# Scan of an RWKV-7 layer: inverses by 16x16 blocks and TensorE, loads and exponentials one pair ahead, 14 chunk tiles

## Chip, cores, metric

The kernel runs on one core of a Trainium2 chip, in float32. The metric is the device time of one execution in microseconds; three executions give the median. The profile is that of one more execution.

## The reference

One inference step of a two-layer trunk: 512 latent tokens and 128 context tokens, width 1024. Layer 0 mixes tokens by a bidirectional RWKV-7 scan, layer 1 by neighbourhood attention; a squared-ReLU MLP follows each. The change touches the scan alone. For each of 16 heads and both directions the reference runs, token by token, on a 64x64 state:

```python
def step(S, inp):
    r_t, w_t, k_t, v_t, kk_t, a_t = inp
    sa = jnp.einsum('bhvk,bhk->bhv', S, -kk_t)
    S_new = (S * w_t[:, :, None, :] + sa[..., None] * (kk_t * a_t)[:, :, None, :]
             + v_t[..., None] * k_t[:, :, None, :])
    y = jnp.einsum('bhvk,bhk->bhv', S_new, r_t)
    return S_new, y
```

## The kernel before, in words

The scan is not run token by token but in chunks of 32. Five steps n = 0 to 4 each take one tile of 128 tokens forward and one backward (n = 0 is the context, the rest the latent tokens); a tile has four chunks, e = 0 to 3. Within a chunk the tokens depend on one another through a lower triangular 32x32 matrix for each head and direction, whose inverse is needed: 128 of them for each n.

**Preparation.** A step n has eight units (half of the heads `hg`, direction `d`, half of the tile `i`; two units with the same `hg` and `d` are a pair). `prep_elem` loads a pair's inputs on SP's queue (lines 890 to 894), makes the running sum of the log decays on DVE (line 896), two exponentials on ACT (897, 898) and products on POOL: KB (912, 913) for the pair, and for each unit a chunk tile C (927). Half of C is filled with zeros first, on ACT (919) and POOL (922), so that a product over all 128 rows picks one head. `prep_group`, twice a unit, multiplies KB by C on TensorE (line 942 by the helper of line 832, tile `pp`), copies the triangular matrices to `invA` (952) and the rest into C (954, 957). After the eighth unit `invert` computes the inverses on DVE (lines 964 to 978): a mask, a transpose of 32x32 blocks, then forward substitution with one multiplication and one addition for each column, split in two from the 11th column on, 100 operations, and a transpose into TT.

**Order.** `fill(k)` does up to k groups, and units as far as there are free C tiles. During the value projection (`tm_product`, line 239) each of 20 output tiles calls `fill(2)`. There are 16 C tiles, eight for even and eight for odd n; twelve of them exist in that stage, so twelve units are done there. In the recurrence `phase_scan` calls `fill` with 0, 1, 1, 2 in each e; two C tiles for each direction come free after every second e.

**Recurrence.** For each n, e and direction `chain_step` does: a state product R on TensorE (16 products of 128x32 tiles, tile A), its copy Rc on ACT (1015), U = TT x Rc on TensorE (16 products of 32x32 tiles), four copies of U into the state tile GU on ACT (1032), the state update on TensorE (16 products of 64x64 tiles, tile B) and its copy on ACT (1088) or with a decay on DVE (1086, 1091), and the output product Y. Once the recurrence runs, every product of helper `mm` (line 832) is tied behind the one before it by a dependency, so TensorE's order there is the order of the program. Between the products stand adaLN products (`adaraw`), whose small addition is line 300 on DVE. Finished tiles are normalised in `post_half`, on DVE, POOL and ACT. After n = 4 `wo_first` begins the output projection (line 1199), with residual buffers `wr` filled on ACT's queue (1195, 1196) and stored on SP's (1202).

The order on DVE, ACT and POOL follows the program as far as a planner's estimate lets it; all four queues run in order.

Of the kernel before, what the change touches and what calls it, by code (L numbers as in the profile page):

```python
# [16 lines left out]
P = 128  # L17
D = 1024
# [154 lines left out]
class K:  # L173
# [534 lines left out]
    def c_slots(self, pool, n, par):  # L708

        for i in range(n):  # L710
            c = pool.tile([P, 26, 64], F32, name=f"C{i}")
            self.nc.any.tensor_copy(c[:, 16:18, :].rearrange("p a x -> p (a x)"), self.cst("ident"))
            self.free[par].append(c)

    def scan_pools(self, st):
        pool = lambda name, bufs, **k: self.pool(st, name, bufs, **k)
        self.ld = pool("ld", 1, side="right")
        self.el = pool("el", 2, side="right")
        self.kbp = pool("kbp", 4, side="right")
        self.ttp = pool("ttp", 2, side="right")  # L720
        self.inv = pool("inv", 1, side="right")
# [9 lines left out]
        self.free = [[], []]  # L731
# [4 lines left out]
        self.steps = [{"tiles": t, "C": {}, "par": i % 2} for i, t in enumerate(((4, 4), (0, 3), (1, 2), (2, 1), (3, 0)))]  # L736
# [3 lines left out]
        self.pin = False  # L740

# [11 lines left out]
    def phase_scan(self, st):  # L753
        nc, tc = self.nc, self.tc
        if True:
# [32 lines left out]
            for n, ts in enumerate(self.steps):  # L788
                for e in range(4):
                    s0, s1 = (self.chain_step(ts, n, e, d) for d in range(2))  # L790
# [72 lines left out]
    def fill(self, n):  # L863

        for i in range(n + 1):
            while self.e_i < len(self.units) and self.e_i <= self.m_i + 2 and self.free[self.units[self.e_i][0]["par"]]:
# [12 lines left out]

    def prep_elem(self, ts, hg, d, i):  # L880

        nc = self.nc
        if "FC" not in ts:
            ts["FC"] = self.fcp.tile([P, 2, 2, 2, 4], F32, name="FC")
        ww = (i, 1 - i)[d]
        tt = ts["tiles"][d]
        rev = (lambda a: a[:, :, :, ::-1]) if d else (lambda a: a)
        if i == 0:
            wi = self.el.tile([P, 520], F32, name="wi")
            nc.sync.dma_start(wi, self.tz_d[d][tt, :, hg])  # L890
            dd = self.ld.tile([P, 1024], F32, name="ld_d")
            nc.sync.dma_start(dd, self.dd_d[d][tt, :, hg])
            sh = self.ld.tile([P, 1024], F32, name="ld_s")
            nc.sync.dma_start(sh, self.sh_d[tt, :, hg])
            w = self.el.tile([P, 520], F32, name="w")
            nc.vector.tensor_tensor_scan(wi, self.cst("scan1"), wi, 0.0, ALU.mult, ALU.add)
            nc.scalar.activation(w, wi, AF.Exp, scale=-0.5 * EXPM)
            nc.scalar.activation(wi, wi, AF.Exp, scale=0.5 * EXPM)
            w, wi = (a.rearrange("p (q w t) -> p q w t", w=2, t=65) for a in (w, wi))
            nc.gpsimd.tensor_copy(ts["FC"][:, d, :, :, 2 * hg:2 * hg + 2].rearrange("p w b l -> p l b w"),  # L900
                                  w[:, :, :, 64].rearrange("p (l b) w -> p l b w", b=2))
            self.pe_in = w, wi, dd, sh
# [12 lines left out]
        C = ts["C"][d, hg, ww] = self.free[ts["par"]].pop(0)  # L915
# [652 lines left out]
```

## Time and profile before

| | us |
|---|---|
| median of three executions | 2249.48 (2247.16 to 2249.74) |
| profiled execution, its own time | 2250.36 |
| profiled execution, span | 2248.5 |
| value projection with the first preparation | 302 to 411 of the span |
| recurrence | 411 to 797 |
| first part of the output projection | 798 to 845 |

The span runs from the first to the last instruction of the profiled execution. Engines are named PE (TensorE matmul), PEld (its weight load), DVE (VectorE), ACT (ScalarE), POOL (GpSimd) and SP (SyncE, which issues DMAs). A product in float32 is issued as two instructions.

### The profile page before, as it was taken

Reading aid. Unit: us, or ns where it says so; the run is one execution under the profiler, and the core shown is the slowest. Engines: PE = TensorE matmul, PEld = TensorE weight load, DVE = VectorE, ACT = ScalarE, POOL = GpSimd, SP = SyncE. Lnnn points to the kernel's source line nnn. Section 1 sums busy time; section 2 is a strip of 40 time slices with the busy share of each in tenths; the row PEclk is TensorE's granted clock in tenths of the full one; section 3 lists DMA queues with packets and bytes.
Section 4 is the critical chain, followed back from the end, with each engine's and each line's share of the span. In section 5 each row is a group of like instructions: output and inputs, shape, how many; then the busy total and the mean of one; then the engine's idle time right before and its main releaser. Section 6 shows DMA issues by size and latency. Waiting matters only on the chain.

```text
span 2248.5 us, 44838 instructions
## 1 busy us (share of the span) xinstructions
PE 2007.7 (89%) x18516; PEld 1823.6 (81%) x18516; DVE 1180.0 (52%) x2587; ACT 866.0 (39%) x1735; POOL 463.8 (21%) x558
## 2 busy tenths in 40 slices
PE   5898978757665677999999999999999999999999
PEld 3787877646554566999999998888777999999999
DVE  6847667396687766433333334434566643434342
ACT  3544554356553425413131323221576331313130
POOL 0001257566552323101010110000232210101010
PEclk9897989888888798999999999999899999999999
DMA  6454864444443455323232223433311232222221
GB/s 232 123 154 140 251 204 158 141 149 148 131 130 121 101 181 164 94 75 113 76 104 75 94 75 114 137 116 108 111 58 29 75 123 75 75 76 74 74 75 70
DMA packets 161388, 260.01 MB, mean 116 GB/s; under 512 B 46880, under 2 KB 103328, under 8 KB 161184
## 3 DMA queue, kind: packets, MB, share of 16 engines
q1 hardware_dynamic: 146816, 240.37, 34.2%
q10 hardware_dynamic: 14368, 16.78, 2.3%
q8 instruction: 145, 2.38, 0.4%
q14 instruction: 59, 0.48, 0.1%
HBM read 218.18 MB, written 37.35 MB: 114 GB/s over the span
## 4 chain that ended last, share of the span: by engine, by line
PE 73%; DVE 13%; DMA 6%; ACT 3%; POOL 2%; issue 2%; SPq 1%; ACTq 0%; DVEq 0%; POOLq 0%
PE psl L205 53%; PE psl L239 4%; PE ps L1495 2%; DVE invT L973 2%; DVE invX L976 2%; PE po L1532 2%; PE pp L832 2%; POOL C L927 2%; PE pt L1520 2%; DVE C L957 1%; PE psl L286 1%; DMA ld_s<-scr 1%; PE pp L1199 1%; DMA wi<-scr 1%; PE st L548 1%
## 5 line engine op out<-in xcount | busy, mean ns | idle before, releaser
L191 ACT CAST whi<-wraw 128x1024 fp32r<-128x1024 f32 x179 | 187.2, 1048 | 730.9 <-PE psl L205 702.5
L205 PE MATMUL psl<-xh,whi 128*128 128x320 f32 (+1 forms) x1712 | 419.8, 318 | 20.8 <-ACT whi L191 15.1
L205 PE MATMUL psl<-xl,whi 128*128 128x320 f32 (+1 forms) x1712 | 417.0, 316 | 7.9 <-DVE xl L248 7.9
L205 PE MATMUL psl<-xh,wlo 128*128 128x320 f32 (+1 forms) x1712 | 415.0, 315 | 2.6 <-DVE wlo L193 2.6
L205 PEld LDWEIGHTS psl<-xh,whi 128*128 128x128 f32 x1712 | 295.4, 192 | 39.4 <-ACT whi L191 19.3
L205 PEld LDWEIGHTS psl<-xl,whi 128*128 128x128 f32 x1712 | 296.3, 192 | 13.9 <-DVE xl L248 10.0
L205 PEld LDWEIGHTS psl<-xh,wlo 128*128 128x128 f32 x1712 | 297.1, 192 | 5.2 <-DVE wlo L193 3.0
L1152 DVE SCALAR_TENSOR_TENSOR xres<-psl,mods,xres 128x320 f32<-128x320 f32 (+2 forms) x216 | 81.7, 434 | 305.5 <-PE psl L205 305.5
L1315 POOL TENSOR_TENSOR relu<-relu 128x640 f32<-128x640 f32 x64 | 80.8, 1263 | 753.1 <-ACT relu L1314 736.2
L205 PE MATMUL psl<-hhh,wlo 128*128 128x320 f32 x1024 | 233.5, 309 | 0.0
L205 PE MATMUL psl<-hhh,whi 128*128 128x320 f32 x1024 | 233.2, 309 | 0.0
L205 PE MATMUL psl<-hhl,whi 128*128 128x320 f32 x1024 | 233.2, 309 | 0.0
L193 DVE TENSOR_TENSOR wlo<-wraw,whi 128x1024 fp32r<-128x1024 f32 x179 | 222.5, 1245 | 14.2 <-ACT whi L191 14.0
L205 PEld LDWEIGHTS psl<-hhh,whi 128*128 128x128 f32 x1024 | 171.2, 188 | 0.4 <-issue 0.4
L205 PEld LDWEIGHTS psl<-hhl,whi 128*128 128x128 f32 x1024 | 171.1, 188 | 0.0
L205 PEld LDWEIGHTS psl<-hhh,wlo 128*128 128x128 f32 x1024 | 171.1, 188 | 0.0
L1272 DVE TENSOR_TENSOR relu<-psl,rms_b 128x320 f32<-128x320 f32 x128 | 60.7, 486 | 144.4 <-PE psl L205 143.3
L832 PE MATMUL pp<-C,KB 128*64 128x128 f32 x1280 | 97.6, 298 | 27.2 <-DVE C L957 13.1
L248 DVE TENSOR_TENSOR hhl<-relu,hhh 128x640 fp32r<-128x640 f32 x64 | 53.4, 834 | 127.9 <-ACT hhh L247 127.8
L832 PEld LDWEIGHTS pp<-C,KB 128*64 128x64 f32 x1280 | 79.9, 149 | 41.3 <-issue 20.7
L957 DVE TENSOR_TENSOR C<-pp,cstsb 64x512 f32<-64x512 f32 x80 | 55.1, 689 | 76.5 <-ACT C L954 68.9
L1032 ACT ACTIVATE GU<-A 32x256 f32<-32x256 f32 x160 | 60.0, 375 | 84.3 <-DVE mods L300 51.8
(288 smaller groups left out, 3389.7 us busy)
## 6 DMA issues: line engine op xcount, KB each, us to landing
wraw<-in_mlp_w SPq DMA_DIRECT2D x128, 512.0 KB, 3.5
adaraw<-in_ada_w SPq DMA_DIRECT2D x96, 512.0 KB, 4.9
ld_d<-scr SPq DMA_DIRECT2D x20, 512.0 KB, 4.1
ld_s<-scr SPq DMA_DIRECT2D x20, 512.0 KB, 3.9
bias<-in_bias SPq DMA_DIRECT2D x16, 384.0 KB, 3.5
scr<-ta SPq DMA_DIRECT2D x16, 325.0 KB, 3.5
wi<-scr SPq DMA_DIRECT2D x20, 260.0 KB, 4.5
scr<-bp SPq DMA_DIRECT2D x16, 320.0 KB, 4.6
```

What stands on the lines that cost most here:

```text
L191: nc.scalar.copy(hi, raw)
L193: nc.vector.tensor_tensor(lo, raw, hi.bitcast(F32), op=ALU.subtract)
L205: self.nc.tensor.matmul(ps[g][:, :e - c], lhsT=a[:, k, :], rhs=b[:, c:e], start=(k == 0 and j == 0), stop=(k == n - 1 and j == 2))
L239: nc.tensor.matmul(ps, lhsT=a[:, tc_], rhs=w, start=(k == 0 and j == 0), stop=(k == KT - 1 and j == 2))
L248: (lo_eng or nc.vector).tensor_tensor(xl, src, xh.bitcast(F32), op=ALU.subtract)
L832: r = (op or self.nc.tensor.matmul)(*a, **k)
L927: nc.gpsimd.tensor_tensor(rev(o) if s == 0 else o, v4(sh, s, ww)[hs], f[hs], op=ALU.mult)
L957: nc.vector.tensor_tensor(C[o, 8 * h:8 * h + 8, :], pn[o, :, 0:64], mask[o], op=ALU.mult)
L1032: nc.scalar.activation(gu[64 - 64 * hp:96 - 64 * hp, hp, pp].rearrange("p b v -> p (b v)"), U[32 * q:32 * q + 32, :], AF.Copy, scale=-0.5)
L1152: nc.vector.scalar_tensor_tensor(out[:, a:b], ps[g][:, o:o + b - a], gate[:, k, j:j + 1], x[:, a:b], op0=ALU.mult, op1=ALU.add)
L1272: nc.vector.tensor_tensor(t[:, c], ps[q][:, :HALF], rb[:, c], op=ALU.mult)
L1315: nc.gpsimd.tensor_tensor(t, t, t, op=ALU.mult)
```

## The change

1. `invert` solves only the two 16x16 diagonal blocks on DVE, both in one operation: 14 multiplications and 14 additions. The off-diagonal block comes from TensorE in two rounds of 128 products of 32x32 tiles with 16 columns (`invert_rest`), with a copy on ACT between them and an addition on DVE behind them; one more transpose on DVE and three zero fills on POOL prepare the operands. The rounds are called from `fill`, the first before the third group after the inverse was issued, or else before the first U that needs them.
2. Loads, running sum and exponentials of a pair are issued with the pair before it; the running sums of the pair after next are loaded then, too. The input buffers are doubled.
3. There are 14 chunk tiles (8, 2 and 4), from which any n may take, within limits at the end; the zero halves and their fills go, and the products of KB with C use 64 rows of the array each.
4. In `wo_first` two residual buffers take the place of three.

```diff
     def c_slots(self, pool, n, par):
+        ident = self.cst("ident")
         for i in range(n):
-            c = pool.tile([P, 26, 64], F32, name=f"C{i}")
-            self.nc.any.tensor_copy(c[:, 16:18, :].rearrange("p a x -> p (a x)"), self.cst("ident"))
+            c = pool.tile([P, 25, 64], F32, name=f"C{i}")
+            self.nc.vector.tensor_tensor(c[:, 16], ident[:, :64], ident[:, 64:], op=ALU.add)
...
+    def room(self, ts, hg, d, i):
+        n = ts["n"]
+        first = (0, 1, 1 - i, i, 0)[n]
+        for j in (first,) if n == 4 or n == 3 and i else (first, 1 - first):
+            if self.free[j]:
+                return j
...
-        self.c_slots(self.pool(self.cst1, "c1", 1, side="right"), 4, 1)
+        self.inv = prep("inv", 1)
+        self.kbp = prep("kbp", 4)
+        self.el = prep("el", 2)
+        self.ld = prep("ld", 2)
+        self.c_slots(prep("c1", 1), 2, 1)
...
     def fill(self, n):
...
+            self.invert_on()
             u = self.units[self.m_i]
             self.prep_group(*u, self.m_g)
...
+    def decays(self, p):
...
+        nc.vector.tensor_tensor_scan(tz, self.cst("scan1"), tz, 0.0, ALU.mult, ALU.add)
+        nc.scalar.activation(w, tz, AF.Exp, scale=-0.5 * EXPM)
+        nc.scalar.activation(wi, tz, AF.Exp, scale=0.5 * EXPM)
...
     def prep_elem(self, ts, hg, d, i):
...
+            self.load_rk(p + 1)
+            self.decays(p + 1)
+            self.load_tz(p + 2)
+            self.pe_in = *self.w_in.pop(p), *self.rk_in.pop(p)
...
-        for h in range(2):
-            z = C[64 - 64 * h:P - 64 * h, 8 * h:8 * h + 8, :]
-            if h:
-                nc.scalar.activation(z.rearrange("p a b -> p (a b)"), self.cst("scan1")[64 - 64 * h:P - 64 * h, :512],
-                                     AF.Copy, scale=0.0)
-            else:
-                nc.gpsimd.memset(z, 0.0)
...
-                self.mm(pv[r:r + 64, e, q, :], lhsT=KB[:, q, e].rearrange("p s t -> p (s t)"), rhs=C[:, n:17 + h:16 + h - n, :],
-                        start=True, stop=True, tile_position=(0, r))
+                self.mm(pv[r:r + 64, e, q, :], lhsT=KB[hs, q, e].rearrange("p s t -> p (s t)"), rhs=C[hs, n:17:16 - n, :],
+                        start=True, stop=True, tile_position=(64 * h, r))
...
     def invert(self, ts):
...
+        nc.gpsimd.memset(Xm[:, 16:32, 0:16], 0.0)
+        nc.gpsimd.memset(Dt[:, :, 0:16], 0.0)
...
+        for s in range(1, 15):
+            m = 15 - s
+            t = tmp[:, :2 * m * s].rearrange("p (b m s) -> p b m s", b=2, m=m)
+            nc.vector.tensor_tensor(t, Xd[:, :, s + 1:, s:s + 1].broadcast_to([P, 2, m, s]),
+                                    Xd[:, :, s:s + 1, 0:s].broadcast_to([P, 2, m, s]), op=ALU.mult)
+            nc.vector.tensor_tensor(Xd[:, :, s + 1:, 0:s], Xd[:, :, s + 1:, 0:s], t, op=ALU.add)
+        nc.vector.transpose(ST.rearrange("p n s -> p s n"), Xm.rearrange("p t s -> p s t"))
+        nc.gpsimd.memset(ST[:, :, 16:32], 0.0)
...
+        self.inv_todo = ts, self.invert_rest(Dt, ST, TT)
+        self.inv_wait = 3
+
+    def invert_rest(self, D, ST, TT):
+        nc = self.nc
+        pz = self.pp_tile()
...
+        for n in range(32):
+            for q in range(4):
+                self.mm(z[32 * q:32 * q + 32, n], lhsT=D[32 * q:32 * q + 16, n, :], rhs=ST[32 * q:32 * q + 16, n, 0:16],
+                        start=True, stop=True, tile_position=(32 * q, 32 * q))
+        nc.scalar.copy(ST[:, :, 0:16], z)
+        yield
+        for n in range(32):
+            for q in range(4):
+                qs = slice(32 * q, 32 * q + 32)
+                self.mm(w[qs, n], lhsT=ST[qs, n, :], rhs=TT[qs, n, 16:32], start=True, stop=True,
+                        tile_position=(32 * q, 32 * q))
+        nc.vector.tensor_tensor(TT[:, :, 16:32], TT[:, :, 16:32], w, op=ALU.add)
+
+    def invert_on(self, ts=None):
+        if ts is None:
+            self.inv_wait -= 1
+            if self.inv_todo and self.inv_wait <= 0 and next(self.inv_todo[1], 1):
+                self.inv_todo = None
+        while ts is not None and self.inv_todo and self.inv_todo[0] is ts:
+            if next(self.inv_todo[1], 1):
+                self.inv_todo = None
...
     def chain_step(self, ts, n, e, d):
...
         yield
+        self.invert_on(ts)
         TT = ts["TT"]
...
     def wo_first(self, adp):
...
-            xi = self.wf[min(k % 3, 1)].tile([P, NA], F32, name=f"wr{k % 3}")
+            xi = self.wf[k % 2].tile([P, NA], F32, name=f"wr{k % 2}")
```

## Rows read from the trace of the kernel before

**Rows 1.** Page, part 1: busy us (share of the span) xinstructions.
```profile
PE 2007.7 (89%) x18516; PEld 1823.6 (81%) x18516; DVE 1180.0 (52%) x2587; ACT 866.0 (39%) x1735; POOL 463.8 (21%) x558
```

**Rows 2.** Stretch, us, busy us (instructions) of PE PEld DVE ACT POOL, clock, DMA: stages.
```profile
302.00:411.00 109.00, 93.64 (x882) 86.03 (x886) 73.62 (x158) 48.65 (x118) 71.42 (x98) 0.94 0.52 159
411.00:798.00 387.00, 247.50 (x6309) 199.94 (x6298) 271.50 (x726) 192.15 (x489) 190.61 (x252) 0.81 0.45 134
```

**Rows 3.** Busy times of the recurrence: n = 4, and the sum of all five.
```profile
733.20:797.00 63.80, 37.77 (x986) 32.00 (x982) 42.10 (x105) 27.00 (x61) 22.48 (x21) 0.73 0.41 105
sum 385.50, PE 246.51 PEld 199.31 DVE 270.25 ACT 190.85 POOL 190.15; mean PE 49.30 PEld 39.86 DVE 54.05 ACT 38.17 POOL 38.03
```

**Rows 4.** Busy times of single steps of the recurrence.
```profile
522.70:536.60 13.90, 12.03 (x344) 9.84 (x344) 5.98 (x10) 9.97 (x28) 8.56 (x14) 1.00 0.57 183
606.50:620.40 13.90, 11.97 (x340) 9.72 (x340) 5.59 (x9) 9.97 (x28) 8.65 (x14) 1.00 0.61 189
620.40:646.30 25.90, 14.52 (x340) 12.16 (x340) 22.56 (x64) 12.21 (x33) 10.32 (x17) 0.74 0.33 105
661.80:678.10 16.30, 13.03 (x352) 10.06 (x340) 8.33 (x13) 10.78 (x30) 6.43 (x10) 0.90 0.57 181
678.10:693.60 15.50, 12.18 (x340) 9.81 (x340) 5.77 (x11) 7.59 (x22) 1.04 (x1) 1.00 0.38 121
747.40:760.00 12.60, 8.55 (x268) 7.12 (x270) 11.16 (x32) 4.91 (x12) 1.04 (x1) 0.89 0.19 43
```

**Rows 5.** Timeline: start us, us, engine, line [idle before <-releaser]; two stretches.
```profile
603.67 1.15 PE L832 MATMUL B<-GU,C 64*64 64x64 f32 x32
...
604.75 1.10 PE L832 MATMUL A<-GU,C 128*32 128x64 f32 x64
...
606.96 0.65 PE L832 MATMUL A<-Rc,TT 32*32 32x64 f32 x32 [1.10 <-ACT Rc L1015]
...
614.45 1.97 PE L832 MATMUL pp<-C,KB 128*64 128x128 f32 x32
...
626.00 0.31 DVE L973 TENSOR_TENSOR invT<-invX 128x30 f32<-128x30 f32 x2
...
637.87 1.07 PE L832 MATMUL A<-Rc,TT 32*32 32x64 f32 x32 [9.71 <-ACT Rc L1015]
...
821.43 4.41 PE L1199 MATMUL pp<-wx,ww 128*128 128x384 f32 x24 [1.28 <-DVE wr L1201]
```

**Rows 6.** Waits in the recurrence: engine, line, waited for: us, times, longest.
```profile
ACT GU L1032 <- DVE mods L300: 51.8, 16, 13.0
...
ACT w L897 <- DVE wi L896: 29.2, 5, 11.4
...
PE A L832 <- DVE TT L978: 16.2, 3, 13.0
```

**Rows 7.** Groups in the recurrence: busy us, mean ns of one | idle before.
```profile
L973 DVE TENSOR_TENSOR invT<-invX 128x108 f32<-128x108 f32 (+14 forms) x200 | 61.5, 335 | 0.9
...
L976 DVE TENSOR_TENSOR invX<-invX,invT 128x38 f32<-128x38 f32 (+14 forms) x200 | 59.7, 324 | 1.0
...
L919 ACT ACTIVATE C<-cstsb 64x512 f32<-64x512 f32 x28 | 17.2, 628 | 1.5 <-PE A L832 1.2
...
L922 POOL MEMSET C<- 64x512 f32 x28 | 14.5, 523 | 7.2 <-PE A L832 6.9
...
L978 DVE STREAM_TRANSPOSE TT<-invX 128x1024 f32<-128x1024 f32 x4 | 7.7, 1931 | 0.1
```

**Rows 8.** The same with the shapes kept apart: two shapes of line 973.
```profile
L973 DVE TENSOR_TENSOR invT<-invX 128x90 f32<-128x90 f32 x12 | 4.2, 353 | 0.0
...
L973 DVE TENSOR_TENSOR invT<-invX 128x110 f32<-128x110 f32 x12 | 2.8, 263 | 0.0
```

**Rows 9.** Waits in the stage before the recurrence.
```profile
PE psl L239 <- ACT vhi L228: 8.3, 2, 4.9
```

**Rows 10.** DMA issues: KB each, median us to landing.
```profile
scr<-wr SPq DMA_DIRECT2D x8, 192.0 KB, 3.1
```

More of the change, by code (lines that the diff above doesn't have):

```diff
@@ L729, in scan_pools @@
             self.gu_zero(self.gu[d][0])
[L731 removed]
+        self.free, self.home = [[], []], {}
         self.c_slots(pool("c0", 1, side="right"), 8, 0)
         self.cst1 = st.enter_context(ExitStack())
[L734 removed]
+        prep = lambda name, bufs: self.pool(self.cst1, name, bufs, side="right")
+        self.inv = prep("inv", 1)
[3 more added lines that the diff above has]
+        self.c_slots(prep("c1", 1), 2, 1)
         self.late = False
[L736 removed]
+        self.steps = [{"tiles": t, "C": {}, "n": i} for i, t in enumerate(((4, 4), (0, 3), (1, 2), (2, 1), (3, 0)))]
+        self.pairs = [(s, hg, d) for s in self.steps for hg in range(2) for d in range(2)]
         self.units = [(s, hg, d, i) for s in self.steps for hg in range(2) for d in range(2) for i in range(2)]
@@ L865, in fill @@
         for i in range(n + 1):
-            while self.e_i < len(self.units) and self.e_i <= self.m_i + 2 and self.free[self.units[self.e_i][0]["par"]]:
+            while self.e_i < len(self.units) and self.e_i <= self.m_i + 2 and self.room(*self.units[self.e_i]) is not None:
                 self.prep_elem(*self.units[self.e_i])
@@ L878, in fill, with load_tz, load_rk @@
                     self.invert(u[0])
+    def load_tz(self, p):
+        if p < len(self.pairs):
+            ts, hg, d = self.pairs[p]
+            tz = self.tz_in[p] = self.el.tile([P, 520], F32, name="tz")
+            self.nc.sync.dma_start(tz, self.tz_d[d][ts["tiles"][d], :, hg])
+    def load_rk(self, p):
+        if p < len(self.pairs):
+            ts, hg, d = self.pairs[p]
+            tt = ts["tiles"][d]
+            dd = self.ld.tile([P, 1024], F32, name="ld_d")
+            self.nc.sync.dma_start(dd, self.dd_d[d][tt, :, hg])
+            sh = self.ld.tile([P, 1024], F32, name="ld_s")
+            self.nc.sync.dma_start(sh, self.sh_d[tt, :, hg])
+            self.rk_in[p] = dd, sh
@@ new lines, in decays @@
+    def decays(self, p):
+        nc = self.nc
+        if p >= len(self.pairs):
+            return
+        ts, hg, d = self.pairs[p]
+        if "FC" not in ts:
+            ts["FC"] = self.fcp.tile([P, 2, 2, 2, 4], F32, name="FC")
+        tz = self.tz_in.pop(p)
+        w = self.el.tile([P, 520], F32, name="w")
+        wi = self.el.tile([P, 520], F32, name="wi")
+        nc.vector.tensor_tensor_scan(tz, self.cst("scan1"), tz, 0.0, ALU.mult, ALU.add)
+        nc.scalar.activation(w, tz, AF.Exp, scale=-0.5 * EXPM)
+        nc.scalar.activation(wi, tz, AF.Exp, scale=0.5 * EXPM)
+        w, wi = (a.rearrange("p (q w t) -> p q w t", w=2, t=65) for a in (w, wi))
+        nc.gpsimd.tensor_copy(ts["FC"][:, d, :, :, 2 * hg:2 * hg + 2].rearrange("p w b l -> p l b w"),
+                              w[:, :, :, 64].rearrange("p (l b) w -> p l b w", b=2))
+        self.w_in[p] = w, wi
@@ L880, in prep_elem @@
     def prep_elem(self, ts, hg, d, i):
         nc = self.nc
-        if "FC" not in ts:
-            ts["FC"] = self.fcp.tile([P, 2, 2, 2, 4], F32, name="FC")
+        p = self.e_i // 2
         ww = (i, 1 - i)[d]
-        tt = ts["tiles"][d]
         rev = (lambda a: a[:, :, :, ::-1]) if d else (lambda a: a)
         if i == 0:
[L889 to L902, printed above, removed]
@@ L1051, in chain_step @@
         if e % 2 == 1:
-            self.free[ts["par"]] += [ts["C"].pop((d, hg, ww)) for hg in range(2)]
+            for hg in range(2):
+                c = ts["C"].pop((d, hg, ww))
+                self.free[self.home[id(c)]].append(c)
         yield
```

51 lines of the change are left out of this document (29 added, 22 removed).

## The prediction

> **What bounds the kernel now.** I read the page first: PE is busy for 89% of the span [rows 1]. The busy times by stage show that this share hides a stretch of another kind: in the 109 us in which the value projection runs beside the first scan preparation PE is busy for 93.6 us at a clock of 0.94, in the 387 us of the recurrence for 247.5 us at 0.81, with DVE at 271.5, ACT at 192 and POOL at 191 [rows 2]. No engine fills the recurrence, so it is a chain of waits, and I cut it into its 20 steps, from one copy of R in the forward direction (line 1015) to the next. They add up to 385.5 us, 19.3 us each, of which 63.8 us belong to the last four, n = 4 [rows 3].
>
> The steps are not alike [rows 4]. Four that hold four groups of preparation and no inverse take 13.9, 13.9, 16.3 and 15.5 us; PE is busy for 12.0 to 13.0 us of them and its clock stands at 0.90 to 1.00. The step beside an inverse takes 25.9 us: DVE is busy for 22.6 us of it, PE for 14.5 us with the clock down to 0.74. A step without groups takes 12.6 us. So outside the inverses TensorE's own order sets the pace, and inside them DVE does.
>
> The timeline shows the mechanism once [rows 5]: PE stands still for 9.71 us before the U product at 637.87 us, which then takes 1.07 us for its 32 instructions; the same product at 606.96 us took 0.65 us. The list of waits names the kinds [rows 6]: ACT waits 51.8 us for the small addition of line 300 and 29.2 us for the running sum of line 896, both queued on DVE among the inverse's operations, and everything on ACT (the copies of R, U and the state) is behind those waits; PE waits 16.2 us for TT itself. The four inverses in this stage cost DVE 61.5 + 59.7 = 121.2 us in lines 973 and 976 [rows 7], 30.3 us each for 100 operations.
>
> **The inverse's DVE part.** 100 operations become 28, on 28 to 112 elements each. Forms of this size take 353 and 263 ns (90 and 110 elements, what POOL does beside them included) [rows 8], mean 308: 28 x 0.308 = 8.6 us in place of 30.3. One more transpose costs 1.9 us [rows 7], and an addition of half its elements out of PSUM under 1 us by estimate from it, some 2.7 us together. DVE is relieved of about 19 us per inverse.
>
> **The inverse's new PE part.** Each inverse gets two rounds of 128 products of 32x32 tiles with 16 columns, 256 instructions a round as this dtype is issued twice (as the 32 instructions of 16 products in [rows 5]). No row has 16 columns. With 64 columns the difference between 64 instructions in 1.10 us and 32 in 0.65 us is 14 ns an instruction [rows 5], 3.6 us a round; if time went with the columns it would be 0.9 us; at the lower clock, 1.07 us for 32, it is 8.6 us. I take 64-column prices, since these rows are the nearest: 5 us for the first round (it follows an idle PE, so half of it at the lower clock) and 3.6 us for the second, bounds 0.9 to 8.6 each. The Trainium skill bears on this (TensorEngine Tiling (Array Packing), Instruction Overhead): a product of one column is said to last as long as one of 60. By it the rounds cost the 64-column price and the sum stands; by columns alone, 0.9 us a round, four inverses would be about 27 us cheaper. No run here has shown which.
>
> **The new wait.** Every product of the recurrence is tied into one PE order by hand, and the two rounds now stand in that order, in the step after the inverse was issued. With 14 chunk tiles in place of 16, eight units of a step are ready one step later than now: following the lists of free tiles through the code, the inverse of n+1 is issued at the end of e = 2 instead of e = 1, and round one stands before the third group of e = 3. What is the time between? PE ends the last group of a step at 614.45 + 1.97 = 616.4 us; the same place of the next step is a step of 13.9 us later, less those two groups, 11.9 us after [rows 5]. DVE's first inverse operation starts at 626.00 us, 9.6 us after that group [rows 5]. Then 8.6 us of operations, some 2 us of other DVE work between them, and one transpose of about 2 us: round one can start 22 us after the group, PE is there after 12. I take a wait of 9 us (bounds 0 and 15: the three new POOL zero fills per inverse, some 0.5 us each like those of line 922 [rows 7], can push it, if they queue behind POOL's products). Behind it on PE stand the state product and the U of both directions, so all of it is on the path. Wait, two rounds: 9 + 5 + 3.6 = 17.5 us for each of three inverses; the fourth stands before the first U of n = 4, with a step of 12.6 us in front and nothing between its rounds, 16 us. Sum 68.5 us.
>
> **The steps.** Fifteen steps hold four groups (ten units are ready when the recurrence starts instead of twelve, so the step n = 3, e = 2 gets groups, too). Their price now is the mean of the four, 14.9 us. The zero fills leave, 17.2 us on ACT and 14.5 us on POOL [rows 7], and with them a wait between a free tile and its product; I take 14.5 us, 217.5 us. The step without groups stays at 12.6 us. The last four keep 63.8 us [rows 3] less the wait for TT at their start, some 3.2 us by estimate (16.2 us in three waits, the longest of 13.0 us taken to be another n's [rows 6]): 60.6 us. Sum with the inverses: 217.5 + 12.6 + 60.6 + 68.5 = 359.2 us, against 385.5: 26.3 us less.
>
> **Loads, running sums and exponentials a pair ahead.** Per pair three DMAs on SP, a running sum on DVE, two exponentials on ACT and a copy on POOL move by one pair; on SP they pass the loads of V for the recurrence, the adaLN weights and the loads of the finished chunks. The 29.2 us of ACT behind line 896 [rows 6] is what they can give back; it is inside the excess of the steps above and I don't count it twice. The price is a new one: the exponential's output buffer, two deep, is now that of the pair whose products POOL has just been given, up to four products of some 0.75 us, 3 us on ACT with R's copy behind it. For 15 pairs that is 0 to 45 us if nothing hides it; POOL is busy for only half of this stage [rows 2] and PE needs 12 us a step, so I take 0.
>
> **The smaller edits.** The products of KB with C get half the rows, and a quarter of the array each instead of a half; the state update's 64x64 tiles run in pairs now (32 instructions in 1.15 us) [rows 5], as the 128x64 ones do, so I keep their price. In the stage before, the projection waits 8.3 us for its converted weights [rows 9], part of it while DVE is held by the first inverse; four groups fewer (4 x 0.98 us, half of 1.97 [rows 5]) and two rounds (about 7 us) nearly cancel, so 4 us less, bounds 12 less and 5 more. In the output projection's first part the residual buffers go from three to two: a store lands in 3.1 us [rows 10] and the buffer is wanted again a product of 4.41 us later [rows 5], so nothing; without that cover about 1 us for each of six.
>
> The sum: 26.3 + 4 = 30.3 us less. The profiled execution took 2250.4 us beside its span of 2248.5, 0.9 above the median of 2249.5; 2250.4 - 30.3 - 0.9 = 2219 us.
>
> **Rivals.** (1) More: PE reaches round one when it is ready, and the rounds go by columns. Inverse 8 us, steps 13.9 us as the two best: 208.5 + 12.6 + 60.6 + 32 = 313.7 us, 72 less; with the stage before, 2174 us. For it: the two clean steps. Against: 28 dependent operations and three transposes do not fit into 12 us. (2) Slower: the wait at round one is 15 us, because POOL's zero fills stand behind products that wait for their loads, and the clock has fallen when it ends. The point is 24.5 us per inverse: 217.5 + 12.6 + 60.6 + 4 x 24.5 = 388.7 us, which eats the 3 to 4 us of the stage before. With 15 + 8.6 + 7 = 30.6 us, about 2273 us. (3) No change: the excess only moves from DVE's queue to PE's order, 24 us an inverse, 2249 us. (4) Products of two row tiles of the array into one PSUM bank cannot run together: then each group of KB and C takes twice 0.98 us, 80 groups x 0.98 = 78 us more on PE, 2297 us. The state update's products are such a pair (upper and lower rows of the array, one bank): its 32 instructions take 1.15 us, 36 ns each, while an instruction of 64 columns alone takes 4 x 14 = 56 ns of its tile, as four tiles share the 14 [rows 5]; so two of them do run together, and that speaks against it. The page TensorEngine Tiling (Array Packing) of the Trainium skill states such a rule (Gotcha 1: PSUM Pressure): different row tiles cannot access one bank at the same time. The trace does not bear it out for the state update.
>
> **Chances.** The forecast 0.56 (its own range 2195 to 2240); (1) 0.21; (3) 0.07; (2) 0.13; (4) 0.03. Within 0.2%, 4.5 us, is about what a measurement cannot tell from no change. Faster 0.56 + 0.21 = 0.77, same 0.07, slower 0.16. The range leaves half of (1) and half of (2) and (4) out: 2178 to 2256 us.
>
> **What would show it.** Lines 973 and 976's successors: 140 operations, near 8.6 us an inverse. The two rounds: 256 instructions each, 3 to 5 us, after an idle PE of about 9 us in the step before each n. ACT's waits for the small addition and for the running sum mostly gone. Steps without an inverse near 14.5 us. It is wrong if PE's wait before round one is under 3 or over 17 us, if the groups of KB and C take longer, or if ACT waits for POOL's products.

## The result, and the profile after

The changed kernel takes 2310.58 us (median of four, 2305.83 to 2312.66), the kernel before beside it 2248.95 us: a ratio of 1.0272, interval 1.0254 to 1.029. It is slower by 62 us where 30 us less was forecast. The profiled execution took 2312.66 us, its span is 2310.9 us, 62.4 us longer than before. Cut by TensorE's work: 5.1 us come before the value projection, whose code is unchanged (TensorE's mean clock in the first 100 us is 0.75, before 0.93); 0.4 in the projection; 39.5 in the recurrence (427.6 against 388.1 us); 4.7 from its end to that of the second value projection; 12.6 from there to the end of layer 1's MLP (672.2 against 659.6 us), all of them in the attention itself (152.9 against 140.3 us).

The busy times of the two stages after, columns as in [rows 2]:

```profile
307.00:416.00 109.00, 94.22 (x1312) 87.97 (x1312) 55.73 (x84) 39.84 (x94) 59.62 (x79) 0.91 0.49 148
416.00:844.00 428.00, 286.29 (x8460) 236.81 (x8459) 214.67 (x452) 185.09 (x476) 180.74 (x249) 0.76 0.39 119
```

DVE has lost 57 us of work in the recurrence, where 4 x 19 = 76 us were forecast, and TensorE has gained 39 us at a lower clock. Four single steps of it, beside [rows 4]: the first one (n = 0, e = 0), one with both rounds, one with groups alone, one without groups.

```profile
416.90:447.40 30.50, 16.86 (x348) 10.95 (x348) 4.71 (x7) 11.61 (x29) 17.94 (x29) 0.78 0.59 174
...
481.00:519.70 38.70, 21.34 (x852) 18.57 (x852) 22.74 (x46) 10.02 (x27) 13.43 (x22) 0.65 0.27 85
...
641.10:654.50 13.40, 11.70 (x340) 9.58 (x340) 4.16 (x7) 8.33 (x24) 10.45 (x16) 1.00 0.37 124
...
795.80:806.90 11.10, 8.58 (x250) 6.75 (x252) 5.19 (x11) 4.94 (x14) 1.04 (x1) 0.86 0.21 49
```

The last two, clean ones, are as forecast (14.5 and 12.6 us). The three steps with rounds take 38.7, 39.3 and 36.4 us. The other twelve with groups add up to 214 us, where 12 x 14.5 = 174 us were forecast. The first took 18.9 us before and takes 30.5, but the second takes 16.1 us where it took 24.8. For n = 0 to 4 the recurrence takes 23 and 14 us more than before, the same, 15 less and 17 more.

The groups on DVE in the recurrence (line 1022 multiplies, 1024 adds; 928 is the running sum), beside [rows 7]:

```profile
L1022 DVE TENSOR_TENSOR invS<-invX 128x28 f32<-128x28 f32 (+6 forms) x56 | 17.5, 313 | 1.7
L1024 DVE TENSOR_TENSOR invX<-invX,invS 128x28 f32<-128x28 f32 (+6 forms) x56 | 17.2, 307 | 1.7
L928 DVE TENSOR_TENSOR_SCAN tz<-cstsb,tz 128x520 f32<-128x520 f32 x10 | 12.5, 1246 | 54.2 <-DMA tz<-scr 54.2
```

(17.5 + 17.2) / 4 = 8.7 us an inverse. The timeline of TensorE around the two rounds of n = 1:

```profile
498.97 2.03 PE L851 MATMUL pp<-invS,invA 16*32 16x16 f32 x135 [10.51 <-DVE C L1002]
502.56 1.80 PE L851 MATMUL pp<-invS,invA 16*32 16x16 f32 x121 [1.55 <-issue]
...
507.43 1.79 PE L851 MATMUL pp<-TT,invS 32*32 32x16 f32 x119
510.11 1.90 PE L851 MATMUL pp<-TT,invS 32*32 32x16 f32 x128 [0.89 <-issue]
514.11 0.33 PE L851 MATMUL pp<-TT,invS 32*32 32x16 f32 x9 [2.10 <-issue]
```

All eight rounds of the recurrence ran at a granted clock of 0.50. An instruction of 16 columns takes 15 ns there (1.90 us for 128). In the same step and at the same clock 32 instructions of 64 columns on tiles of the same size take 1.07 us, 33 ns each (at a clock of 1.00, in [rows 4] and [rows 5], they took 0.65 us, 20 ns):

```profile
776.03 1.90 PE L851 MATMUL pp<-TT,invS 32*32 32x16 f32 x128 [0.68 <-issue]
788.59 1.07 PE L851 MATMUL A<-Rc,TT 32*32 32x64 f32 x32 [7.07 <-DVE TT L1049]
```

```profile
776.00:778.00 2.00, 1.90 (x128) 1.79 (x128) 1.76 (x8) 0.00 (x0) 0.00 (x0) 0.50 0.80 291
788.60:789.60 1.00, 1.00 (x33) 0.83 (x33) 0.90 (x4) 0.00 (x0) 0.00 (x0) 0.50 0.08 2
```

From the start of one instruction to the start of the next the trace has 13.5 ns with 16 columns and 24.8 ns with 64 at 0.50.

A round is broken by stops of 0.5 to 3 us; the first round takes 5.3 to 6.9 us, the second 5.8 to 7.0. From one stop to the next TensorE takes 256 instructions, weight loads counted (once 255, twice 511). Each stop ends 1.3 to 1.6 us after a transfer of 16384 bytes in the queue of instructions has landed; five of these fall into 498 to 516 us, one into the same stretch before:

```profile
q8 instruction: 5, 0.08, 1.7%
```

So TensorE seems to wait there for its own instructions, 16384 / 256 = 64 bytes each; no run tried it. In front of the first round TensorE stands for 10.51 us. The list of waits, beside [rows 6]:

```profile
DVE tz L928 <- DMA tz<-scr: 54.2, 10, 10.9
...
ACT wi L930 <- POOL C L971: 51.0, 6, 14.4
...
ACT GU L1113 <- DVE mods L300: 36.6, 12, 9.1
```

The wait for line 300 fell from 51.8 us; two new ones came.

### The profile page after: what moved, and what is told of

Read it like the earlier page. It is cut to its first block, busy times and chain, and to the rows that moved or that the text cites. A ratio compares the mean times of both kernels' runs of the same rounds, so it can differ in the third digit from the quotient of the medians.

```text
span 2310.9 us, 49609 instructions
## 1 busy us (share of the span) xinstructions
PE 2059.1 (89%) x21076; PEld 1869.1 (81%) x21076; DVE 1104.5 (48%) x2243; ACT 847.0 (37%) x1692; POOL 438.5 (19%) x533
## 4 chain that ended last, share of the span: by engine, by line
PE 74%; DVE 9%; DMA 6%; issue 5%; POOL 3%; ACT 2%; SPq 1%; ACTq 0%; DVEq 0%; POOLq 0%
PE psl L205 52%; PE psl L239 4%; PE pp L851 4%; PE ps L1578 3%; POOL C L971 2%; PE po L1615 2%; PE pt L1603 2%; DMA tz<-scr 2%; PE B L851 1%; PE A L851 1%; PE pp L1282 1%; PE psl L286 1%; DVE invS L1022 1%; DVE C L1002 1%; DVE invX L1024 1%
## 5 line engine op out<-in xcount | busy, mean ns | idle before, releaser
L205 PE MATMUL psl<-xl,whi 128*128 128x320 f32 (+1 forms) x1712 | 417.2, 316 | 10.5 <-DVE xl L248 10.5
L205 PEld LDWEIGHTS psl<-xh,whi 128*128 128x128 f32 x1712 | 295.4, 192 | 39.1 <-ACT whi L191 17.2
L851 PE MATMUL pp<-C,KB 64*64 64x128 f32 x1280 | 99.8, 301 | 25.7 <-DVE mods L300 7.7
L248 DVE TENSOR_TENSOR hhl<-relu,hhh 128x640 fp32r<-128x640 f32 x64 | 53.3, 833 | 127.9 <-ACT hhh L247 127.8
L851 PEld LDWEIGHTS pp<-C,KB 64*64 64x64 f32 x1280 | 80.9, 149 | 39.5 <-issue 17.9
L1113 ACT ACTIVATE GU<-A 32x256 f32<-32x256 f32 x160 | 59.9, 374 | 63.0 <-DVE mods L300 36.6
## 6 DMA issues: line engine op xcount, KB each, us to landing
bias<-in_bias SPq DMA_DIRECT2D x16, 384.0 KB, 3.5
```

What stands on the lines that cost most here:

```text
L205: self.nc.tensor.matmul(ps[g][:, :e - c], lhsT=a[:, k, :], rhs=b[:, c:e], start=(k == 0 and j == 0), stop=(k == n - 1 and j == 2))
L248: (lo_eng or nc.vector).tensor_tensor(xl, src, xh.bitcast(F32), op=ALU.subtract)
L851: r = (op or self.nc.tensor.matmul)(*a, **k)
L1113: nc.scalar.activation(gu[64 - 64 * hp:96 - 64 * hp, hp, pp].rearrange("p b v -> p (b v)"), U[32 * q:32 * q + 32, :], AF.Copy, scale=-0.5)
```

## The experiments

Stages are cut by TensorE's first and last products. "Recurrence" is 388.1 us in the kernel before and 427.6 us in the changed one. Ratios are to the kernel before on the same chip. Undoing a part lets the planner lay out all queues anew, which turned out to matter.

**One part of the change undone.** e1 puts the inverse of before back, e2 the loads, running sums and exponentials, e3 delays the rounds, e5 leaves them out, and with them the off-diagonal blocks of the inverses.

```diff
-        self.inv_todo = ts, self.invert_rest(Dt, ST, TT)
-        self.inv_wait = 3
+        self.inv_wait = 99
```

(e5 without the first line alone, e3 with the wait of 99 alone; e1 and e2 take `invert` and the first lines of `prep_elem` from the kernel before, e2 with one input buffer.)

> The changed kernel with the inverse of before (100 operations on DVE, no rounds on TensorE); chunk tiles and the work made a pair ahead stay as changed. Theory A (the loss is the rounds: 256 products each, pinned in PE's order one step after a later inverse, so that PE waits in front of them; 20 to 25 us of excess per inverse): an inverse then costs the 11 us of excess it had before, 4 x 12 = about 50 us less than the changed kernel, near 2262 us. Theory B (the loss is the running sum issued a pair ahead: DVE stands at it until its DMA has landed and everything behind it, the small additions and with them ACT's copies of U, is late; ACT's exponentials wait for POOL's products): DVE gets 80 us of work more in the same queue and the steps beside stay long, so no gain, 2305 to 2340 us. Theory C (part of the loss, 12.6 us, is TensorE's clock in the attention, whose code is the same): the attention's stretch, 672 us in the changed kernel and 660 us before, goes by the clock and not by this edit.

> The changed kernel with loads, running sum and exponentials back beside the products of their own pair (one buffer of inputs, as before); inverse by blocks, rounds and 14 chunk tiles stay. Theory A: nothing of the loss goes, 2300 to 2320 us. Theory B: the twelve steps with groups and without an inverse, which add up to 214 us in the changed kernel, come down to about 15 us each, so 30 to 40 us less, 2270 to 2280 us; DVE's wait for the DMA of the running sum and ACT's wait for POOL's products, 54 and 51 us in the list of waits, go down to the level of before.

> The changed kernel with both rounds as late as they can be, in front of the first U of the next n, so that DVE has long ended its 28 operations. Theory A: the 8 to 11 us that PE waits for round one go; the rounds stay (some 12 us) with the copy between them bare (some 2 us), so about 7 us less for each of three inverses in the recurrence, near 2290 us. Theory B: the wait in front of round one overlapped with DVE's lateness and turns up elsewhere, within 5 us of the changed kernel, 2306 to 2316 us.

> The changed kernel without the two rounds, the copy between them and the addition behind them: the off-diagonal 16x16 block of every inverse is left out. Everything else, DVE's 28 operations among it, stays. Theory A: the whole excess of the inverses goes, 80 to 100 us, 2210 to 2230 us. Theory B: only the rounds' own time goes, 4 x 12 us, about 2265 us, and the waits of DVE for its DMA and of ACT for POOL stay at 50 us each.

Measured: e1 2304.9 us (ratio 1.0235, 1.0194 to 1.0276; recurrence 438.3 us), e2 2318.4 (1.0285, 1.0242 to 1.0329; 441.6), e3 2312.55 (1.0283, 1.0242 to 1.0323; 438.3), e5 2267.32 (1.0073, 1.0042 to 1.0104; 380.8). Neither A nor B holds alone: the inverse or the loads of before make it no faster. The rounds cost 47 us of recurrence. In e5 the four steps that held rounds take 25.3, 27.0, 22.9 and 17.6 us against 38.7, 39.3, 36.4 and 34.5: 14 us each. And the wait in front of round one is not the rounds' alone: at the same place of e5's timeline the next group of KB and C waits as long, for its PSUM tile, whose evacuation (line 1002) stands on DVE behind the inverse's operations.

```profile
489.60 3.68 PE L851 MATMUL pp<-C,KB 64*64 64x128 f32 x32 [10.51 <-DVE C L1002]
```

**What is left without both parts.** e6 undoes the inverse and the loads together; e8 has 16 tiles, the new inverse and the loads of before; e10 is the kernel before with the layout of C alone; e9 reorders the work made a pair ahead.

```diff
-                self.mm(pv[r:r + 64, e, q, :], lhsT=KB[:, q, e].rearrange("p s t -> p (s t)"), rhs=C[:, n:17 + h:16 + h - n, :],
-                        start=True, stop=True, tile_position=(0, r))
+                self.mm(pv[r:r + 64, e, q, :], lhsT=KB[hs, q, e].rearrange("p s t -> p (s t)"), rhs=C[hs, n:17:16 - n, :],
+                        start=True, stop=True, tile_position=(64 * h, r))
```

(e10, beside C of 25 columns with its preset on DVE, and without the zero fills.)

> The changed kernel with both the inverse of before and the loads, running sums and exponentials of before: what is left of the change is the stock of 14 chunk tiles, C without zero halves and the products of KB with 64 rows. Theory A or B, each part alone to blame (rounds or pair-ahead work): with both undone the time is that of before or less, 2235 to 2255 us. Theory D (14 tiles instead of 16: eight units of a step are ready later, so the inverse stands one chunk closer to the U that needs it, and a pair's loads are no longer covered by waiting units): the recurrence stays at 430 to 440 us as in the changed kernel without either part, 2295 to 2315 us.

> 16 chunk tiles in the stock (8, 4 and 4), with the inverse by blocks and its rounds, and the loads and exponentials of before, which leaves the room for the two tiles. The same with 14 tiles took 2318 us and 442 us in the recurrence. Theory D: two tiles give back the 40 to 50 us, recurrence 385 to 400 us, 2255 to 2275 us. Theory A: the rounds cost their 14 us each wherever they stand and the wait before them stays, recurrence over 425 us, about 2300 us.

> The kernel before with one part of the change: C without zero halves and their fills, and the products of KB with C over 64 rows in two row tiles; 16 tiles by even and odd n, loads and inverse of before. All theories: 17.2 us on ACT and 14.5 us on POOL go, the groups on PE keep their price; ACT and POOL stand behind waits for half of this stage, so 0 to 15 us less than before, 2235 to 2250 us. If the two row tiles hurt (products of two row tiles into one bank), the groups take longer and it is slower, over 2260 us.

> The changed kernel with the pair-ahead work in another order: the load for the running sum is issued before the two other loads, which wait for their buffers, and running sum and exponentials are issued half a pair later, behind the first unit's products, so that the exponential's buffer is that of products further back in POOL's queue. Theory B: DVE's 54 us of waiting for that load and ACT's 51 us for POOL's products go down by half or more; the step in which the recurrence begins falls from 30.5 to about 20 us; 20 to 35 us less in all, 2275 to 2290 us. Theory A or D: the waits move and the time stays within 8 us of the changed kernel.

Measured: e6 2305.66 us (1.0237, 1.0193 to 1.028; recurrence 445.9), e8 2331.43 (1.0354, 1.0309 to 1.0399; 445.4), e9 2310.15 (1.0252, 1.0203 to 1.0302; 432.6, DVE still waits 54.9 us and ACT 53.3). And e10, which removes 31.7 us of work from the recurrence and adds none: 2303.73 us (1.023, 1.0188 to 1.0272), recurrence 429.6. So one edit, which I had costed at nothing, is enough for a loss nearly as large as the changed kernel's. Two more tiles give nothing back in e8, which speaks against theory D.

**Where in the layout, and the wait for the load.** e11 puts the fills back into e10. e15 issues the running sum's load from ACT's queue, e16 makes the small addition of line 300 on ACT in the changed kernel, e17 in the kernel before.

```diff
-            self.nc.sync.dma_start(tz, self.tz_d[d][ts["tiles"][d], :, hg])
+            self.nc.scalar.dma_start(tz, self.tz_d[d][ts["tiles"][d], :, hg])
...
-        nc.vector.tensor_tensor(m, pm.rearrange("p (k j) -> p k j", j=2), ab.unsqueeze(2).broadcast_to([P, 2, 2]), op=ALU.add)
+        for k in range(2 if mm else 0):
+            nc.scalar.activation(m[:, k], pm[:, 2 * k:2 * k + 2], AF.Identity, bias=ab[:, k:k + 1])
+        if not mm:
+            nc.vector.tensor_tensor(m, pm.rearrange("p (k j) -> p k j", j=2), ab.unsqueeze(2).broadcast_to([P, 2, 2]), op=ALU.add)
```

(`mm` is given in the recurrence alone.)

> The kernel with the layout alone (2304 us), with the zero fills on ACT and POOL put back as work without use: the halves they fill are written again by the evacuation of the group. Theory E (what costs is the place of the running sum in DVE's order, in front of the small addition of line 300 whose end ACT's copies of U wait for, while its load has not landed): the order on DVE is nearly that of the layout alone, running sum first, so the loss stays, 2290 to 2315 us, in spite of or because of 31.7 us of fills more. Theory F (the missing fills are the cause, since POOL and ACT run ahead into other waits): back to 2245 to 2260 us.

> The changed kernel with the load of the running sum's input issued from ACT's queue instead of SP's, where it stands behind loads that wait for a free buffer and behind the loads of finished chunks. Theory E: DVE's 54 us of waiting for this load go to under 15 us, the 10 us stall of the first step (30.5 us) goes, steps with groups come down to 14 to 16 us, 20 to 35 us less: 2275 to 2290 us. Theory A (rounds) or D (14 tiles): the wait is filled by the next one, within 8 us of the changed kernel, 2303 to 2318 us.

> The changed kernel with the small addition of line 300 in the recurrence made on ACT, as two activations with a bias, in place of DVE, so that ACT's copies of U no longer wait for DVE's queue. Theory E: the 36.6 us of ACT's wait go, less what the evacuations of the groups, which stand behind the same running sum, take in their place, and 16 x 2 activations of some 0.25 us, 8 us, come on ACT: 15 to 30 us less, 2280 to 2295 us. Theory A or D: within 8 us of the changed kernel.

> The kernel before with the same edit alone: the small addition of line 300 on ACT. Theory E: ACT's 51.8 us of waiting for it go, part of them is taken over by PE's wait for the evacuations behind the same queue: 15 to 30 us less than before, 2220 to 2237 us. If these waits only cover others, within 8 us of before, 2241 to 2257 us.

Measured: e11 2306.4 us (1.0236, 1.0193 to 1.0279): the fills are not it, theory F falls. e15 2311.61 (1.0244, 1.0186 to 1.0302; DVE's wait 52.7 us): taking the load off SP's queue does not bring it earlier. e16 2299.91 (1.0209, 1.0166 to 1.0252): the first step falls from 30.5 to 20.5 us, so its stall did come through line 300, but the next two grow from 16.1 and 17.5 to 20.8 and 20.1 us, and the recurrence falls by 1.3 us only, to 426.3. The rest of what e16 gains lies outside it, in code that the edit leaves as it is: in the profiled executions 7.4 us before the value projection and 9.8 us behind the second one. e17 2256.53 (1.0022, 0.9995 to 1.0048): in the kernel before, the same wait covers others. Why a copy of U should wait for an addition that only reads another part of its PSUM tile: the page PSUM — Partial Sum Buffer of the Trainium skill, section PSUM bank collisions raise a hardware error, tells of a compiler's scheduler that adds a dependency between two instructions on different engines that touch the same bank and the same 32 partitions, reads too. The trace agrees that the copies wait: in the first step of the changed kernel those of the backward direction start within 0.03 us of line 300's end (441.24 us after 441.07 + 0.14). Whether the bank is the reason, or the tile as a whole, no run here shows.

**The products or the order.** e21 has the one statement above alone, with C of 26 columns and its fills. In e22 the same program's five queues are tied, each instruction behind the one before it, into the order of the kernel before; in e25 the program before is tied into the order of e21 (with the preset of each C tile on the engine that it has there); e23 is e22 without the fills.

```diff
         K(nc, tc, aps).run()
+        pin_order(nc, tc)
...
+    for names in json.loads(zlib.decompress(base64.b64decode(ORDER))):
...
+        for a, b in zip(have, have[1:]):
+            tc.add_manual_dep(b, a.name, mybir.DependencyInfo(
+                mybir.DependencyClass.NoSync, mybir.DependencyReason.DATA), reason="order")
```

> The kernel before with one statement changed: the products of KB with C run over 64 rows each, in two row tiles (C keeps its 26 columns, zero halves and fills). Theory G (the loss comes with these products: the planner, which lays out the queues by its own estimate of times, lays them out otherwise when they change, and the running sums come to stand ahead of the small additions): the whole loss is here already, 2295 to 2315 us. Theory H (another edit of the layout, the preset of C made on DVE, holds the loss): 2240 to 2258 us.

> The same products over 64 rows, but the order of all five queues written out by hand as it is in the kernel before, instruction by instruction. Theory G in its first form (order alone): the loss is gone, 2240 to 2256 us. Theory I (the products themselves: row tiles in one bank, or a TensorE clock that falls with less of the array in use): the loss stays, 2285 to 2310 us.

> The counterpart: the products of the kernel before, over 128 rows, with the order of all five queues as it is in the kernel with products over 64 rows. Theory G (order alone): the loss appears without any change of the work, 2290 to 2312 us. Theory I (the products): no loss, 2240 to 2258 us.

> Products over 64 rows and no zero fills (the 80 fills on ACT and POOL are left out, and nothing reads what they wrote), all other instructions in the order of the kernel before. Theory G: the gain that the layout was good for comes out, 0 to 15 us less than before, 2233 to 2252 us. Theory I: over 2280 us.

| | order of before | order laid out for 64 rows |
|---|---|---|
| products over 128 rows | before: 2248.82 us | e25: 2303.52 us, 1.0249 (1.0228 to 1.027) |
| products over 64 rows | e22: 2248.91 us, 1.0006 (0.9984 to 1.0027) | e21: 2300.28 us, 1.0241 (1.0208 to 1.0274) |

Of this statement the order is the whole effect, the products have none; e23 takes 2247.03 us (1.0, 0.9967 to 1.0032), so the fills, 31.7 us of work in the recurrence, were free. Three steps (n = 0, e = 0; n = 0, e = 2; n = 1, e = 2) and the recurrence by busy times, e22 first, then e25:

```profile
405.50:426.20 20.70, 16.68 (x348) 11.38 (x348) 2.92 (x5) 12.33 (x32) 14.91 (x23) 0.84 0.63 188
448.70:466.20 17.50, 11.72 (x340) 9.61 (x340) 16.89 (x31) 11.78 (x31) 12.73 (x18) 1.00 0.49 158
531.00:553.70 22.70, 13.53 (x340) 11.80 (x340) 22.32 (x45) 12.79 (x34) 17.64 (x21) 0.83 0.58 180
404.80:793.20 388.40, 248.96 (x6346) 202.66 (x6345) 275.47 (x728) 192.78 (x490) 191.91 (x252) 0.82 0.44 134
```

```profile
411.30:447.50 36.20, 17.29 (x348) 11.94 (x348) 4.67 (x7) 13.46 (x33) 19.84 (x31) 0.72 0.51 155
461.40:490.30 28.90, 15.99 (x339) 13.52 (x340) 27.62 (x81) 11.91 (x31) 12.84 (x18) 0.71 0.36 114
555.30:589.30 34.00, 16.61 (x324) 13.97 (x328) 33.51 (x105) 12.82 (x33) 19.59 (x23) 0.76 0.40 126
410.60:845.00 434.40, 266.03 (x6345) 213.74 (x6344) 270.42 (x726) 195.82 (x492) 186.64 (x252) 0.78 0.39 120
```

The counts of instructions agree within two on every engine; TensorE's 17 us more come with a lower clock, 0.78 for 0.82. The step behind the first is shorter in e25, 13.9 us for 22.5. What the order does is seen on ACT's timeline at the same chunk, first in e25 (its line numbers are two higher), then in the kernel before:

```profile
464.76 0.37 ACT L289 COPY adasb<-pp 128x256 f32<-128x256 f32 x1
476.06 0.64 ACT L899 ACTIVATE w<-wi 128x520 f32<-128x520 f32 x1 [10.93 <-DVE wi L898]
476.79 0.64 ACT L900 ACTIVATE wi<-wi 128x520 f32<-128x520 f32 x1
477.43 1.06 ACT L954 COPY invA<-pp 32x128 f32<-32x128 f32 x4
...
478.98 0.38 ACT L1017 COPY Rc<-A 128x256 f32<-128x256 f32 x1
```

```profile
458.60 0.37 ACT L289 COPY adasb<-pp 128x256 f32<-128x256 f32 x1
460.01 1.06 ACT L952 COPY invA<-pp 32x128 f32<-32x128 f32 x4 [1.04 <-DVE invX L965]
...
461.57 0.38 ACT L1015 COPY Rc<-A 128x256 f32<-128x256 f32 x1
...
468.81 0.64 ACT L897 ACTIVATE w<-wi 128x520 f32<-128x520 f32 x1 [0.28 <-DVE wi L896]
```

In the new order an exponential stands ahead of the copies of the group and of R and waits 10.93 us for its running sum, and the recurrence with it; before, it stood behind them and waited 0.28 us. In the list of waits over the recurrence ACT's wait for the running sum is 29.2 us before [rows 6], and TensorE's wait for ACT's copies of U, in front of the state update, is the first line here; then both in e25:

```profile
PE B L832 <- ACT GU L1032: 6.7, 6, 2.8
...
ACT w L899 <- DVE wi L898: 59.9, 6, 15.2
...
PE B L834 <- ACT GU L1034: 30.4, 11, 15.0
```

**One instruction, and a version meant to beat both.** e36 is the kernel before in its own order, but for three running sums on DVE, each in front of one small addition more, where the new order has them. e40 is the layout in the order of before; the room of the narrower C holds a third buffer for running sums, and six of their loads move forward on SP.

```diff
-        self.el = pool("el", 2, side="right")
+        self.el = pool("el", 3, side="right")
```

> The kernel before, its products and the order of its queues written out by hand, but for three instructions on DVE: three running sums (those that the order of the kernel with products over 64 rows moves so) stand in front of one small addition of line 300 that they stood behind, in the steps n = 0, e = 0; n = 0, e = 2; n = 1, e = 2. Theory G with its mechanism (running sum waits for its load, small addition behind it, ACT's copies of U behind that): these three steps, 18.9, 17.5 and 22.7 us in the kernel before, take 28 to 35 us each, 25 to 40 us more in all, 2272 to 2292 us. Rival J (it takes the orders of several queues together, and DVE alone finds its way): under 2260 us.

> A version meant to beat both: the layout alone (C of 25 columns, no fills, products over 64 rows) in the order of the kernel before; the room that the narrower C leaves holds a third buffer of running sums, and six loads of the running sums' input in the recurrence move forward on SP, behind the load of products of two pairs before. Theory G: DVE's wait for these loads, 18.7 us in the kernel before, of which 10.3 us stand in the step n = 0, e = 1 (24.9 us), goes for the most part; 5 to 15 us less than before, 2233 to 2244 us. Rival: other waits take their place, 2244 to 2256 us.

e36: 2255.6 us, 1.0019 (1.0 to 1.0039). The first three steps, and n = 1, e = 2, by the busy times:

```profile
413.40:447.70 34.30, 17.05 (x348) 11.51 (x348) 5.20 (x7) 12.30 (x32) 19.66 (x31) 0.75 0.55 163
447.70:461.40 13.70, 11.71 (x340) 9.59 (x340) 5.33 (x9) 10.89 (x29) 9.29 (x16) 1.00 0.46 147
461.40:480.10 18.70, 12.89 (x340) 10.46 (x340) 17.27 (x33) 11.77 (x32) 12.19 (x17) 0.91 0.55 179
543.30:564.90 21.60, 13.71 (x340) 11.68 (x340) 20.85 (x44) 12.79 (x33) 14.83 (x19) 0.84 0.50 157
```

The first step grows from 18.9 to 34.3 us, but the next falls from 24.8 to 13.7: it is one wait for one load, met earlier. The other two moves change about 1 us each. So the running sums on DVE are not enough (rival J holds); that the exponentials on ACT make the rest is read from e25's timeline and was not tried alone. e40: 2245.74 us, 0.9975 (0.9955 to 0.9995), 5 us less than before and hardly more than the interval can tell, recurrence 384.0 us, where e23 without the third buffer has 385.2; DVE's wait for the loads went only from 18.7 to 16.0 us, so the rival's times came.

## Why the prediction was wrong

- **DVE's part of the inverse**: right, 8.7 us for 8.6. What it replaces was put too high: lines 973 and 976 overlap in the trace, and together they keep DVE busy for 110.9 us, 27.7 us an inverse, not 30.3.
- **The rounds**: the price of the products came out right by luck. I took 64 columns at the full clock, 3.6 us a round, and half of the first at the lower one; the products are busy for 3.9 and 4.0 us a round, with 16 columns, all at a clock of 0.50. Two misses cancel. By the page TensorEngine Tiling (Array Packing) of the Trainium skill, section Instruction Overhead, 16 columns would last as long as 60; the trace does not agree, 13.5 ns against 24.8 ns for 64 at the same clock. By columns alone it would be a quarter, which is not so either. The term was mis-sized by the stops inside a round: 5.8 + 6.5 us for 5 + 3.6, and 14 us a step when the rounds are taken out.
- **The wait in front of round one**: 10.5, 11.5 and 8.1 us for 9, near in size and the cause only in part. I had it end when the inverse is ready, which in n = 1 is the case at 496.3 us; round one begins 2.7 us later, when its `pp` tile is free, whose evacuation stands behind the inverse on DVE. e5 shows the group behind it waiting as long for that tile. An inverse with everything came to 22 to 25 us of excess (steps of 36.4 to 39.3 and of 34.5 us, less 14.5 and 12.6), at the break-even of 24.5 us that rival (2) named.
- **"I take 14.5 us" for fifteen steps**: this is the step that failed. The steps of the changed kernel add up to 425 us, cut as in the prediction, where its sum has 359.2. Of these 66 us 40 stand in the twelve steps with groups and without rounds, which take 17.8 us each; 18 stand in the three with rounds, 4 in n = 4 and 3 in the step n = 3, e = 3. I priced the steps by the best four of the old order. But before there are six steps with four groups and no inverse, and the two that I left out, n = 0, e = 0 and e = 1, take 18.9 and 24.8 us:

```profile
411.50:430.40 18.90, 15.05 (x348) 10.97 (x348) 2.92 (x5) 12.31 (x32) 13.97 (x22) 0.91 0.65 189
430.40:455.20 24.80, 13.54 (x340) 11.07 (x340) 8.21 (x11) 10.88 (x29) 17.14 (x26) 0.86 0.55 174
```

In the second DVE waits 10.3 us for the load of a running sum and ACT 11.4 us for that sum. The mean of the six is 17.2 us, which puts fifteen steps 41 us above 217.5. So it does not hold that TensorE's order sets the pace outside the inverses, and this could be read before any run. Nor does the old order stay: e21, e22 and e25 show that the one statement in `prep_group`, which does not change the time of its products, makes the planner lay out every queue anew, and that this alone costs 43 to 46 us of recurrence (431.2 and 434.4 us against 388.1). That a planner's estimate sets the order stood in my own description of the kernel; I did not price it.
- **Pair-ahead work**: the price that I took as 0, with a bound of 45 us, shows as 51.0 us of ACT's wait for POOL, one of the signs of being wrong that I had named, and DVE's wait for the load came on top. What they cost is not shown: neither could be taken out alone with a gain (e2, e9, e15).
- **The smaller edits**: the price of the groups was right. An instruction's median by tile, in the changed kernel, is 269 ns, before 273 ns, and e22 takes the time of before; rival (4) is out.

```profile
L851 PE MATMUL pp<-C,KB x960: 269/269/473, 420.4 to 742.3; 64*64 64x128 f32 x192
```

The Trainium skill's rule on row tiles in one bank (the page TensorEngine Tiling (Array Packing), Gotcha 1: PSUM Pressure), which stood beside rival (4), is not borne out by this row either.
- **Left out altogether**: the attention's 12.6 us, below.

Open: the changed kernel's own instruction list has no counterpart before, so it was not run in an order of before, and how much of its 39.5 us of recurrence the new order makes is not shown. For the order speak the shared statement and the like size (427.6 and 431.2 us). For the rounds as a rival speaks e5: without them the recurrence takes 380.8 us, less than before. The losses also lie in other places: for n = 0 to 4 e25 takes 22, 9, 7 and 8 us more than before and 1 less, the changed kernel 23, 14 and 0 more, 15 less and 17 more.

## What to carry to other kernels

Where a planner lays out in-order queues by its own estimate, an edit can be two edits: the work, and a new order. Compare the orders first, and measure the edit once with the old order tied down; here the work of one edit was worth nothing and its order over 50 us. What waits for a DMA (a running sum, and the exponential behind it on the next engine) belongs behind the copies that a recurrence waits for, by e25's timeline. A wait's size in a list is no price: e17 took away one of 51.8 us for nothing, e16 one of 36.6 us for 1.3 us of recurrence. And a price by the clean steps of a trace needs all steps of their kind: two of six were left out here.

## What was not expected of the hardware

TensorE's clock in unchanged code. In the attention of the changed kernel, 15 to 55 us behind the second value projection, TensorE is busy without a break and is granted first the lower of its two levels (0.50 is 1.2 GHz), then 0.72; at the same place of the kernel before 0.91 and 1.00. Busy times, after and then before:

```profile
1649.70:1669.70 20.00, 20.00 (x81) 13.71 (x80) 7.73 (x30) 8.91 (x27) 3.65 (x7) 0.50 0.09 31
1669.70:1689.70 20.00, 20.00 (x109) 13.78 (x108) 10.65 (x42) 11.84 (x35) 4.33 (x9) 0.72 0.13 41
```

```profile
1600.00:1620.00 20.00, 20.00 (x135) 14.24 (x134) 12.85 (x53) 14.18 (x45) 6.02 (x11) 0.91 0.18 57
1620.00:1640.00 20.00, 20.00 (x140) 14.38 (x138) 13.31 (x54) 14.26 (x43) 6.75 (x13) 1.00 0.13 40
```

The attention took 153 to 155 us in the changed kernel, e3, e5, e9 and e15, and 138 to 144 us in every other kernel here, in one profiled execution of each; e16, among the latter, has the same scan but for line 300. What decides it stays open; it is a fifth of the changed kernel's loss.
